# Two sets of projections as seven block products instead of eight, with the weight sums formed in the two sets before

## The chip, the cores and the metric

The kernel runs on one core of one Trainium2 chip. The metric is the device time of one execution in microseconds, taken as the median of several runs. A core has five engines with their own instruction streams: TensorE (matmuls from SBUF into PSUM), VectorE and ScalarE (elementwise work, both can read PSUM), GpSimd (elementwise work on SBUF) and SyncE, whose stream here issues nearly all DMAs. The profile calls them PE, DVE, ACT, POOL and SP; PEld is the loading of weights into TensorE.

## The reference

One inference step of a hybrid decoder layer: 2048 new positions of a prompt and 8 x 4 of samples, 1024 channels. A row-normalised input h is projected by one wide matrix, and the columns feed a short convolution and an RWKV-7 recurrence over 16 heads of 64. The two branches go through an output matrix each, are gated and added, and go through a last matrix.

```python
h = _rmsnorm(x, norm_g)
p = jnp.einsum('bsd,dn->bsn', h, w_in)            # 1024 -> 4*1024 + 4*1024 + 128 + 2*1024
xin, bg, cg, zc = _split(p_conv, CONV_SIZES)
u = cg * xin
y_c = bg * conv3(u) * jax.nn.silu(zc)
xm = p_rwkv + (prev - p_rwkv) * mu_shift          # prev: the row before
r, k, v, wd, ad, zr = _split(xm, RWKV_SIZES)
S_fin, ys = _rwkv7_scan(S0, r_h, k_h, v_h, decay, kk, a_h)
y_r = (groupnorm(ys) + bonus) * jax.nn.silu(zr)
m = jax.nn.sigmoid(gc) * (y_c @ w_out_c) + jax.nn.sigmoid(gr) * (y_r @ w_out_r)
out = x + m @ w_o                                 # then a last RMSNorm
```

The large matrices are kept in float32 accuracy by splitting both operands of each product into a high and a low part of the type fp32r: weight-high x input-high, weight-low x input-high and weight-high x input-low are added up in PSUM.

## The kernel before

**Sets.** The prompt is cut into four sets of NT = 512 positions (th = 0 to 3; LAST = 3). The last set also carries the 32 sample positions, and 8 shifted rows for the blocks that need them, so its width is 544 or 552. For a set, XH and XL (L382, L383) hold the high and low part of the normalised input, eight blocks of 128 channels (NB = 8) by the set's positions. `prep` (L749) loads four tiles of x, scales them, transposes them on TensorE and splits them (`to_cols`, L738).

**Blocks.** A `Block` (L451) is one projection to 128 output channels. There are 81 for a set: one for the low-rank inputs (`lora_block`), and for each of eight pairs of heads k, r, v, z (`rkvz_blocks`, L1002) and xin, cg, zc, bg, gc, gr (`conv_blocks`, L874). `proj` (L434) adds eight channel blocks times three split terms, 24 matmuls, into one PSUM bank of the pool ps_ip (three banks). Sets one to three do this with 512 moving columns; set four runs each block twice, with 256 and with 288 or 296 columns, as a bank holds 512. The first and last three blocks of a set run in halves as well (EDGE), so that the input of the next set can be prepared under them. The block's `evac` then reads the bank with ScalarE and VectorE.

**Weights.** In set one a weight block is loaded as 512 KB into one of four wraw buffers, ScalarE casts the high part into a whl buffer, VectorE subtracts to get the low part (`w_advance`, L390; `w_lows`, L414), and the pair of 1 MB goes back to DRAM. Sets two to four load that 1 MB straight into one of four whl buffers. `take_w` (L423) hands out the weights in the order in which the plan uses them and keeps the loads up to four blocks ahead.

**Side work.** Beside the blocks run the steps of the recurrence for each pair of heads: `rwkv_keys`, `rwkv_solve`, `rwkv_merge`, `rwkv_load`, `rwkv_chain` (eight chunks of 64, each waiting for the one before; PSUM pools ps_a with two banks, ps_b with one, ps_t with two), for the last set `rwkv_sequences`, and `rwkv_out`. Each is a generator with a kind and a stretch of the main stream over which it is spread. While the program is built, a model of the engines (`Clock`, L58) says when operands are ready, and `Side.run` (L493) lets a step go only then. So the order of each engine is fixed when the program is built, and on the chip it is only waited for. SP issues in that order too: a DMA that waits holds back those behind it.

**Merges.** Under the end of set four `merge_first` (L1497) multiplies the convolution outputs of sets one and two by w_out_c, with `load_first` (L1523) splitting them into XH and XL. Then, for each set, the remaining products with w_out_c and w_out_r and the last product with w_o follow, with weights kept in the same way.

The profile gives one line for every recorded operation, L264, because all engines are called through one helper; groups are told apart by the names of their tiles: ip is a ps_ip bank, whl a weight pair, pa, pb and pt banks of the side work.

## Time and profile before

| what | us |
|---|---|
| median of 3 runs (3165.68 to 3173.09) | 3166.51 |
| span of the profiled execution | 3166.9 |
| TensorE busy in it | 3071.6 |
| VectorE busy | 1972.5 |
| ScalarE busy | 1256.6 |
| GpSimd busy | 316.2 |

DMA moved 621.89 MB, 196 GB/s over the span. The span is that of one execution taken by the profiler; it lies 0.4 us above the median. Busy times of matmuls overlap, so a busy TensorE is not one at its peak. In a row of a group stand the engine, the operation, output and input tiles, shapes and count, then the busy time, the mean of one in ns, and the idle time of that engine just before, with what ended it. In a row of a stretch stand its length and the busy time of TensorE, its weight loads, VectorE, ScalarE and GpSimd, then TensorE's granted clock, the busy share of the DMA engines and GB/s.

### The profile page before, as it was taken

How to read it: one execution, taken by the hardware profiler on the slowest of the kernel's cores; microseconds unless marked ns; L12 is line 12 of the kernel's file. 1: busy time of each engine (PE TensorE's matmuls, PEld its weight loads, DVE VectorE, ACT ScalarE, POOL GpSimd, SP SyncE). 2: the span in 40 equal slices, each digit the busy share in tenths (PEclk: the TensorE clock that was granted, in tenths of full speed). 3: DMA queues.
4: the chain of work that ended last, by engine and by line, in shares of the span. 5: the costliest groups of instructions: out<-in, count | busy, mean ns of one | idle time of the engine just before them, and what ended most of it. 6: DMA issues, size and time to landing. Idle time of an engine off the chain costs nothing. (4 is left out here: it accounts for less than half of the span.)

```text
span 3166.9 us, 55564 instructions
## 1 busy us (share of the span) xinstructions
PE 3071.6 (97%) x21530; PEld 2630.7 (83%) x21530; DVE 1972.5 (62%) x5444; ACT 1256.6 (40%) x2583; POOL 316.2 (10%) x521
## 2 busy tenths in 40 slices
PE   7899999999999999999999999999999998999998
PEld 6678777888888888787888889998999988878896
DVE  5577777766666666666656676777677753443432
ACT  4455555544343444444444444444444431211201
POOL 2011111111111111111111110000000010000000
PEclk9899999999999999999999999999999999999999
DMA  8677777754444444444444444443444469988863
GB/s 269 234 241 234 227 226 227 239 192 162 151 164 166 166 163 162 163 163 151 161 164 164 159 152 138 149 141 131 147 148 136 165 226 313 346 324 316 315 240 120
DMA packets 252253, 621.89 MB, mean 196 GB/s; under 512 B 35210, under 2 KB 153091, under 8 KB 198230
## 3 DMA queue, kind: packets, MB, share of 16 engines
q1 hardware_dynamic: 251846, 617.82, 56.9%
q8 instruction: 170, 2.79, 0.3%
q14 instruction: 93, 0.76, 0.1%
q0 software_dynamic: 144, 0.52, 0.0%
HBM read 457.34 MB, written 160.94 MB: 195 GB/s over the span
## 5 line engine op out<-in xcount | busy, mean ns | idle before, releaser
L264 PE MATMUL ip<-XH,whl 128*128 128x512 f32 (+3 forms) x7776 | 2112.6, 352 | 34.3 <-DVE tmp L264 11.0
L264 PEld LDWEIGHTS ip<-XH,whl 128*128 128x128 f32 x7776 | 1346.6, 191 | 190.2 <-DVE whl L264 12.2
L264 PE MATMUL ip<-XL,whl 128*128 128x512 f32 (+3 forms) x3888 | 1364.7, 351 | 0.1
L264 PEld LDWEIGHTS ip<-XL,whl 128*128 128x128 f32 x3888 | 741.5, 191 | 74.5 <-issue 5.6
L264 DVE TENSOR_TENSOR tt<-Mi,X 128x60 f32<-128x60 f32 (+24 forms) x992 | 215.3, 217 | 29.9
L264 DVE TENSOR_TENSOR X<-X,tt 128x60 f32<-128x60 f32 (+24 forms) x992 | 211.7, 213 | 32.3
L264 DVE SCALAR_TENSOR_TENSOR S<-pb,pe,sp 64x64 f32<-64x64 f32 x512 | 143.6, 280 | 135.7 <-PE pb L264 128.3
L264 ACT ACTIVATE tmp<-ip,vec 128x512 f32<-128x512 f32 (+2 forms) x174 | 102.6, 592 | 281.0 <-PE ip L264 276.7
L264 ACT ACTIVATE sp<-S,pe 128x128 f32<-128x128 f32 x256 | 102.8, 402 | 265.0 <-DVE S L264 264.1
L264 ACT COPY SV<-pb 64x128 f32<-64x128 f32 x256 | 66.0, 258 | 325.0 <-PE pb L264 323.0
L264 PE MATMUL po<-whl,MH 128*128 128x512 f32 x544 | 170.4, 394 | 0.0
L264 DVE TENSOR_TENSOR UB<-pa,P 64x64 f32<-64x64 f32 x512 | 109.9, 215 | 95.8 <-PE pa L264 78.9
L264 DVE TENSOR_TENSOR whl<-wraw,whl 128x1024 fp32r<-128x1024 f32 x105 | 132.8, 1267 | 50.5 <-ACT whl L264 42.1
L264 ACT CAST whl<-wraw 128x1024 fp32r<-128x1024 f32 x105 | 108.9, 1040 | 58.9 <-PE ip L264 36.9
L264 PE MATMUL ip<-RH,whl 128*128 128x512 f32 (+2 forms) x512 | 128.4, 342 | 2.1 <-DMA whl<-w_or 1.9
L264 PEld LDWEIGHTS po<-whl,MH 128*128 128x128 f32 x544 | 102.3, 188 | 23.6
L264 ACT COPY Xbd<-Mi 32x256 f32<-32x256 f32 x128 | 88.2, 689 | 72.0 <-DVE Mi L264 69.8
L264 DVE SCALAR_TENSOR_TENSOR gt<-gt,ip 128x288 f32<-128x288 f32 (+2 forms) x67 | 36.5, 544 | 125.4 <-PE ip L264 100.8
L264 ACT ACTIVATE tmp<-ip 128x512 f32<-128x512 f32 (+2 forms) x126 | 63.0, 500 | 124.3 <-PE ip L264 124.0
L264 PEld LDWEIGHTS pb<-UB,Xbd 128*128 128x128 f32 x512 | 86.7, 189 | 30.5 <-PE ip L264 9.2
L264 PEld LDWEIGHTS pa<-S,AR 128*128 128x128 f32 x512 | 89.9, 190 | 26.5 <-DVE S L264 12.1
L264 DVE TENSOR_TENSOR GM<-pt,mask_p 128x512 f32<-128x512 f32 x128 | 82.6, 686 | 45.8 <-PE pt L264 45.6
(495 smaller groups left out, 3914.4 us busy)
## 6 DMA issues: line engine op xcount, KB each, us to landing
wraw<-in_w_in_dram SPq DMA_DIRECT2D x81, 512.0 KB
whl<-w_k SPq DMA_DIRECT2D x24, 1024.0 KB
whl<-w_r SPq DMA_DIRECT2D x24, 1024.0 KB
whl<-w_v SPq DMA_DIRECT2D x24, 1024.0 KB
whl<-w_z SPq DMA_DIRECT2D x24, 1024.0 KB
whl<-w_xin SPq DMA_DIRECT2D x24, 1024.0 KB
whl<-w_cg SPq DMA_DIRECT2D x24, 1024.0 KB
whl<-w_zc SPq DMA_DIRECT2D x24, 1024.0 KB
```

Of the source, the lines that this page charges most:

```text
L264: r = f(*a, **k)
```

## The change

Sets three and four (FAST = (2, 3)) no longer multiply block by block. Two blocks X and Y of 128 outputs, the 1024 input channels in two halves and the positions in two halves make a product of 2 x 2 by 2 x 2 blocks. Eight products of (128 outputs) x (512 channels) x (half of the positions) are replaced by seven, in the manner of Strassen and Winograd: four of them use sums S1 to S4 of weight blocks, four use sums T1 to T4 of input blocks, and three of these use both. A product is 4 channel blocks x 3 split terms, 12 matmuls with 256 columns in set three and 276 in set four (XN). The 81 blocks of a set become 40 pairs and a lora block of 60 matmuls.

- `Pair.product` runs the products of a pair in seven of the slots that SLOTS gives, with those of neighbouring pairs between. m, b and c are PSUM banks; m takes P1, P6, P7 and P4 one on top of the other and is read after each of them. Passes on ScalarE and VectorE put the four output quarters together, and the former evacuation work runs once both blocks are whole (`mixed_fin`, `inner_end`, `outer_end`, `gates_end`; `outer_end` multiplies by bg on GpSimd).
- The unit of weights is half a block, 512 KB with both parts, and whl has seven such buffers in place of four of 1 MB.
- `comb` makes the sums of weights: 12 pairs beside set one and 28 beside set two. It reloads both raw blocks, adds on GpSimd, splits on ScalarE and VectorE and stores four units.
- `xprep` makes the seven parts of a set's input (VARS) one set ahead and stores them in DRAM; `load_x_part` brings each part to its place (PLACE) as soon as the last product that reads the old one is issued. T1, T3, T4 and B22 lie in XA, the former XH and XL; B11, B21 and T2 in six of the raw buffers, of which there are now eight.
- ps_ip has four banks in place of three, and ps_a one in place of two. The last stage's pools, the order of a few small steps (new_shift, new_conv, the buffers of `rwkv_sequences`) and constants of the model change along with it. The split of the first half of yc no longer starts under the end of set four.

The core of the diff:

```diff
+NUNIT = 7
+FAST = (2, 3)
+SLOTS = {"P1": 0, "P2": 1, "P6": 3, "P5": 5, "P7": 6, "P4": 9, "P3": 11}
+HOLDS = {"P1": "B11", "P2": "B21", "P6": "T2", "P5": "T1", "P7": "T3", "P4": "T4", "P3": "B22"}
...
-    whl_p = clock.pooled(ctx.enter_context(tc.tile_pool(name="whl", bufs=4)), "whl", 4)
+    whl_p = clock.pooled(ctx.enter_context(tc.tile_pool(name="whl", bufs=NUNIT)), "whl", NUNIT)
...
-        w_advance(i + 3, i + 2, i + WAHEAD)
-        return parts_.pop(i)
+        w_advance(i + 6, i + 4, i + NUNIT)
+        return [parts_.pop(i + j) for j in range(n)]
...
-    ps_a = clock.pooled(ph1.enter_context(tc.tile_pool(name="ps_a", bufs=2, space=PSUM)), "ps_a", 2)
+    ps_a = clock.pooled(ph1.enter_context(tc.tile_pool(name="ps_a", bufs=1, space=PSUM)), "ps_a", 1)
...
+    def load_x_part(th, v):
...
+        if isinstance(at, int):
+            t = XA[:, at * NB * XW // 2:at * NB * XW // 2 + NB * n].rearrange("p (a k t) -> p a k t", a=2, t=n)
+            SP.dma_start(out=t.bitcast(F32), in_=src)
+            xv[v] = t[:, 0], t[:, 1]
+        else:
...
+            for i in range(2):
+                SP.dma_start(out=xv[v][i].bitcast(F32), in_=src[:, i])
...
+    def xprep(th):
...
+            t1, t2, t4 = (xt[:, i * n:(i + 1) * n] for i in range(3))
+            V.tensor_tensor(out=t1, in0=b11, in1=b12, op=ALU.subtract)
+            V.tensor_tensor(out=b12, in0=b22, in1=b12, op=ALU.subtract)
+            V.scalar_tensor_tensor(out=t2, in0=t1, scalar=-1.0, in1=b22, op0=ALU.mult, op1=ALU.subtract)
+            V.scalar_tensor_tensor(out=t4, in0=t2, scalar=-1.0, in1=b21, op0=ALU.mult, op1=ALU.subtract)
+            yield 1, [t4]
+            for vi, src in enumerate((b11, b12, b21, b22, t1, t2, t4)):
+                hi = rw.tile([P, XW // 2], F32R, name="xhi")[:, 0:n]
+                A.copy(hi, src)
+                V.tensor_tensor(out=src.bitcast(F32R), in0=src, in1=hi.bitcast(F32), op=ALU.subtract)
+                yield 0.5, [src, hi]
+                SP.dma_start(x_d[th][:, vi, 0, k, :], hi.bitcast(F32))
+                SP.dma_start(x_d[th][:, vi, 1, k, :], src)
...
+        def product(self, k):
...
+            u, = take_w((self.th, *self.unit(k)), 1)
+            v = HOLDS[k]
...
+            ps = self.b if k == "P2" else self.c if k in ("P5", "P3") else self.m
+            u = u.rearrange("p a (k n) -> p a k n", n=P)
+            xh, xl = xv[v]
+            for kt in range(HB):
+                for i, (w_, m_) in enumerate(((u[:, 0, kt], xh[:, kt]), (u[:, 1, kt], xh[:, kt]), (u[:, 0, kt], xl[:, kt]))):
+                    T.matmul(ps[:, :n], lhsT=w_, rhs=m_, start=kt + i == 0 and k in ("P1", "P2", "P5"),
+                             stop=kt == HB - 1 and i == 2, skip_group_check=k in ("P6", "P7", "P4", "P3"))
+                    yield n / NT / 3
+            X, Y = self.x, self.y
+            if k == "P1":
+                A.copy(X[:, h], ps[:, :n])
+            elif k == "P2":
+                V.tensor_tensor(out=X[:, h], in0=ps[:, :n], in1=X[:, h], op=ALU.add)
+                ps_ip.free(ps)
+            elif k == "P6":
+                A.copy(X[:, e], ps[:, :n])
+            elif k == "P7":
+                A.copy(Y[:, e], ps[:, :n])
+                V.scalar_tensor_tensor(out=Y[:, e], in0=self.c[:, :n], scalar=-1.0, in1=Y[:, e], op0=ALU.mult, op1=ALU.subtract)
+            elif k == "P4":
+                A.activation(out=Y[:, h], in_=ps[:, :n], func=AF.Copy, scale=-1.0)
+                ps_ip.free(ps)
+            elif k == "P3":
+                V.tensor_tensor(out=X[:, e], in0=ps[:, :n], in1=X[:, e], op=ALU.add)
+                ps_ip.free(ps)
+                self.end(X, Y)
...
+    def comb(prs, me, ahead, spare):
...
+            adds = [(u1, Y[:, h], Y[:, e]), (Y, X[:, h], Y[:, h]), (u2, u1[:, e], X[:, h]), (X, u2[:, e], X[:, e])]
+            for t, a, b in adds[0:2]:
+                G.tensor_tensor(out=t[:, e], in0=a, in1=b, op=ALU.add)
...
+            for two in (((1, u1), (3, Y)), ((2, u2), (4, X))):
+                for _, t in two:
+                    A.copy(t[:, h].bitcast(F32R), t[:, e])
+                yield 1, [t[:, h] for _, t in two]
+                for _, t in two:
+                    V.tensor_tensor(out=t[:, e].bitcast(F32R), in0=t[:, e], in1=t[:, h], op=ALU.subtract)
+                more(i)
+                yield 1, [t[:, e] for _, t in two]
+                for k, t in two:
+                    SP.dma_start(flat((f"S{k}", *pr.names[0])), t)
+                    wraw_p.free(t)
```

More of the change, by code (lines that the diff above doesn't have):

```diff
@@ L400, in w_advance @@
             i = state["split"]
-            _, src, keep, there = order[i]
-            if i >= (load if there else split):
+            _, j, src, keep, there = order[i]
+            if i >= min(load if there else split, state["dma"]):
                 break
-            hl = whl_p.tile([P, 2, NB * P], F32R, name="whl")
+            hl = whl_p.tile([P, 2, UW], F32R, name="whl")
             if there:
@@ L517, in push @@
     def push():
+        SP.flush(0)
+        if tmp.open:
+            return
         for sd in [sd for kind in ("samp", "keys", "out") for sd in live if sd.kind == kind and sd.f0 <= where[0]]:
-            if all(x.ended for x in sd.after):
+            if not sd.running and all(x.ended for x in sd.after):
                 sd.run(where[0] + 1e-6, True, True)
@@ L1540, in load_first, with units, do, g @@
             yield 1
-    EDGE = 3
+    def units(bl):
+        kind = (bl.key[0],) + bl.key[2:]
+        return [(bl.key, kind + (j,), j, bl.src) for j in range(2)]
+    def do(f, *a):
+        def g():
+            f(*a)
+            return
+            yield
+        return 0.0, g, ()
+    def product(pr, k):
+        u = pr.unit(k)
+        j = u[-1] if k in ("P1", "P2", "P4") else 0
+        return 4.0 * pr.n / NT, lambda: pr.product(k), [((pr.th, *u), u, j, None)]
+    def lora_item(th):
+        bl = lora_block(th)
+        a, c = units(bl)
+        return 60.0 * XN[th] / NT / 3, lambda: lora_fast(bl, XN[th], NTT[th]), [a, (bl.key, ("ln",), 0, None), c]
@@ new lines, in block_item, with g, items, length @@
+    def block_item(x, c0, c1):
+        def g():
+            kind = (x.key[0], x.key[1]) if x.key[0] in ("oc", "or") else ("prep", x.key[1])
+            need(*(job.get((*kind, hf)) for hf in range(2) if (c1 > HN if hf else c0 < HN)))
+            yield from x.part(c0, c1)
+        return (c1 - c0) / NT * NB, g, units(x)
+    def items(parts):
+        return [block_item(*x) for x in parts]
+    def length(its):
+        return sum(w for w, _, _ in its)
+    EDGE = 3
+    F0 = FAST[0]
+    blocks = {th: [x for b in range(NB) for x in conv_blocks(th, b)] for th in range(NSETS) if th not in FAST}
@@ new lines, in hybrid_kernel, with rested @@
+    for pr in pairs:
+        for k in ("P5", "P6", "P7", "P3"):
+            kind = pr.unit(k)
+            if kind not in scratch:
+                scratch[kind] = dram.tile([P, 2, UW], F32, name="w_" + "_".join(map(str, kind)))
+    scratch["ln",] = dram.tile([P, 2, UW], F32, name="w_ln")
+    for _, hv, _, _ in plan:
+        for _, _, us in hv:
+            for u in us:
+                keep(*u)
+    def rested(n):
+        return sum(wraw_p.ends(h) + REST <= clock.t["PE"] for h in wraw_p.open) >= n
@@ L1694, in hybrid_kernel @@
     before = None
+    sums = [pr for pr in pairs if pr.th == F0]
+    seldom = {0: sums[:12], 1: sums[12:]}
     clock.planning = True
```

525 lines of the change are left out of this document (390 added, 135 removed).

## The prediction

> **What bounds the kernel now.** First the head of the profile's page.
>
> ```profile
> span 3166.9 us, 55564 instructions
> PE 3071.6 (97%) x21530; PEld 2630.7 (83%) x21530; DVE 1972.5 (62%) x5444; ACT 1256.6 (40%) x2583; POOL 316.2 (10%) x521
> ...
> PEclk9899999999999999999999999999999999999999
> ```
>
> TensorE is busy for 97% of the span at nearly full granted clock. That alone proves little, so I cut the span by stage: start, set one, set two, set three, set four, first merge, rest. The boundaries are where the 1944 projection matmuls of 512 columns of a set (81 blocks of 24) are used up.
>
> ```profile
> core 0: us, PE busy (x) PEld busy (x) DVE busy (x) ACT busy (x) POOL busy (x), PEclk, DMA share, GB/s
> 0.00:130.00 130.00, 102.70 (x511) 84.75 (x512) 74.22 (x155) 65.11 (x103) 22.72 (x71) 0.96 0.82 273
> 130.00:647.00 517.00, 506.23 (x3342) 408.43 (x3342) 394.05 (x1000) 268.99 (x498) 68.89 (x93) 0.99 0.72 229
> 647.00:1251.00 604.00, 595.88 (x4063) 491.40 (x4062) 386.61 (x1128) 250.06 (x521) 69.71 (x118) 1.00 0.47 162
> 1251.00:1854.00 603.00, 594.21 (x4051) 489.78 (x4051) 385.42 (x1120) 250.14 (x520) 70.94 (x118) 1.00 0.47 161
> 1854.00:2574.00 720.00, 706.62 (x6415) 665.33 (x6413) 506.69 (x1608) 313.61 (x747) 64.32 (x100) 1.00 0.43 147
> 2574.00:2700.00 126.00, 114.10 (x849) 107.20 (x849) 50.81 (x86) 27.90 (x38) 6.15 (x4) 0.95 0.89 310
> 2700.00:3167.00 467.00, 451.89 (x2312) 383.79 (x2310) 174.72 (x350) 80.75 (x158) 13.50 (x17) 0.99 0.75 275
> ```
>
> Sets three and four (rows 1251 and 1854) leave TensorE idle for 8.8 and 13.4 us; VectorE, the next compute engine, is at 64 and 70% there, and the DMA engines are below half. A matmul taken out of these two rows shortens the span as long as nothing else fills up. The waits of TensorE over the whole span say the same: none adds up to 15 us.
>
> ```profile
> engine line waited for: us in total, times, longest us
> PE ip L264 <- DVE tmp L264: 14.9, 10, 8.0
> PE ip L264 <- DVE GM L264: 10.7, 1, 10.7
> PE ip L264 <- DVE whl L264: 9.6, 8, 3.5
> ```
>
> **The matmuls removed.** A matmul's busy time overlaps its neighbour's, so the price is the distance of starts in the timeline of TensorE, for 512, 296 and 256 columns:
>
> ```profile
> 1505.57 0.62 PE L264 MATMUL ip<-XH,whl 128*128 128x512 f32 x2
> ...
> 1508.37 0.63 PE L264 MATMUL ip<-XH,whl 128*128 128x512 f32 x2
> ...
> 2207.36 0.44 PE L264 MATMUL ip<-XH,whl 128*128 128x296 f32 x2
> ...
> 2208.18 0.44 PE L264 MATMUL ip<-XH,whl 128*128 128x296 f32 x2
> ...
> 2208.59 0.40 PE L264 MATMUL ip<-XH,whl 128*128 128x256 f32 x2
> ...
> 2209.65 0.28 PE L264 MATMUL ip<-XH,whl 128*128 128x256 f32 x1
> ```
>
> Twelve of 512 take 2.80 us (233.3 ns), six of 296 take 0.82 us (136.7 ns), nine of 256 take 1.06 us (117.8 ns). The line through 256 and 296 gives 133 ns at 288 and 127.3 ns at 276, the width in set four afterwards.
>
> Set three before: 1944 x 233.3 = 453.5 us. After: 40 pairs x 7 products x 12 matmuls, and 60 for the lora block, 3420 x 117.8 = 402.9 us. Set four before: each block is a part of 256 and one of 296 (33 blocks) or 288 (48), 1944 x (117.8 + 134.5) = 490.5 us. After: 3420 x 127.3 = 435.4 us. The gain is 50.6 + 55.1 = **105.7 us**. The transposes of x move from prep to xprep, 32 a set in both; no recurrence matmul changes. Nothing lies under these matmuls that could be uncovered at once: the next bounds are DMA and VectorE.
>
> The Trainium skill (TensorE: Matmul & The Clock Gate, Back-to-back issue gap) speaks against this: it says the spacing is set by the weight load as well as the matmul, with 81 ns at 128 columns and 131 ns at 512. A line through these would put 256 at 98 ns, 0.75 of the 512 figure, an estimate from that page; then 84 narrow matmuls would cost as much as 63 wide ones in place of 48 and the change would lose. The trace disagrees for this type: 117.8 of 233.3 ns is 0.505.
>
> **What is added, and its cover.** Prices of elementwise work, from the groups by form:
>
> ```profile
> L264 DVE SCALAR_TENSOR_TENSOR tmp<-tmp,ip 128x256 f32<-128x256 f32 x32 | 13.1, 418 | 30.5 <-PE ip L264 15.6 <-DMA tmp<-gc 12.6 <-ACT tmp L264 2.2
> L264 ACT ACTIVATE tmp<-ip 128x256 f32<-128x256 f32 x36 | 13.8, 383 | 30.3 <-PE ip L264 30.1
> L264 DVE SCALAR_TENSOR_TENSOR ML<-gt,MH 128x512 fp32r<-128x512 f32 x21 | 14.5, 691 | 12.0 <-ACT MH L264 12.0
> L264 POOL TENSOR_TENSOR tmp<-tmp,bv 128x512 f32<-128x512 f32 x24 | 30.9, 1286 | 87.5 <-ACT tmp L264 87.5
> L264 ACT CAST whl<-wraw 128x1024 fp32r<-128x1024 f32 x105 | 108.9, 1040 | 58.9 <-PE ip L264 36.9 <-DMA wraw<-in_w_o_dram 8.3 <-DMA wraw<-in_w_out_r_dram 6.8
> ```
>
> Each pair adds three VectorE and four ScalarE passes of 256 columns: 40 x 3 x 0.418 = 50 us and 40 x 4 x 0.383 = 61 us a set. The bg multiply goes to GpSimd (-5.5 us of VectorE). Set four drops the second part of its evacuations, about 72 instructions, each worth 2 x 0.418 - 0.69 = 0.15 us (-11 us). The sums cost 4 x 0.69 us of VectorE and 4 x 1.286 us of GpSimd a weight pair: 33 and 62 us for 12 pairs in set one, 77 and 144 us for 28 pairs in set two; xprep's 44 passes at 0.418 us stand against prep's twelve at 0.69, some 10 us more in sets two and three. VectorE's share becomes 427/517 = 0.83, 474/604 = 0.78, 440/554 = 0.79, 536/665 = 0.81 in sets one to four (before 0.76, 0.64, 0.64, 0.70).
>
> What does a busier VectorE cost TensorE? In the stage rows TensorE idles 1.4% where VectorE is at 0.64, 1.9% at 0.70 and 2.1% at 0.76, 6 points for 100. At the new shares that is +2, +5, +5 and +4 us, **16 us**; between 0 (the planner places work ahead) and 30 (twice the slope, GpSimd's adds taking their turns with VectorE).
>
> DMA. A unit is 512 KB; a whole block was 1 MB:
>
> ```profile
> wraw<-in_w_in_dram SPq DMA_DIRECT2D x81, 512.0 KB
> whl<-w_k SPq DMA_DIRECT2D x24, 1024.0 KB
> ...
> 80.00:100.00 20.00, 15.97 (x62) 12.04 (x61) 8.93 (x12) 9.29 (x15) 0.39 (x3) 0.91 1.00 359
> 2880.00:2920.00 40.00, 39.84 (x172) 31.72 (x171) 13.09 (x19) 4.55 (x8) 0.00 (x0) 1.00 0.83 306
> 2920.00:2960.00 40.00, 40.00 (x174) 32.39 (x173) 13.83 (x21) 6.24 (x11) 0.00 (x0) 1.00 0.86 322
> ```
>
> Set three moves 161 x 603 = 97 MB. It loses 81 x 1.05 = 85 MB and gains 283 units = 148 MB, xprep's stores of seven parts (8 MB) and some 12 MB of part loads: 180 MB in 554 us, 326 GB/s. Set two: 98 MB and 28 pairs x (1.05 read + 2.1 written) = 88 MB, parts 10 MB: 196 MB in 604 us, 325 GB/s. Set one: 118 + 12 x 3.15 = 156 MB in 517 us, 302 GB/s. Set four: 169 MB in 665 us, 254 GB/s. From below, the rows at 2880 show 306 and 322 GB/s with TensorE busy for 79.84 of 80 us. From above, the first merge at 310 GB/s has TensorE idle 9.4% of the time, 8% more than a set. Loads straight from scratch make up set three and the rows at 2880 alike, so I take 1% of sets two and three and half that of set one: **14 us**, ends 0 and 0.08 x 1675 = 134.
>
> The Trainium skill (DMA: Bandwidth & Descriptors, Specifications) gives about 358 GB/s of HBM bandwidth a core. By it sets two and three would sit at 91% of the limit, an estimate from that page, and nothing would be lost on average; the trace agrees as far as it goes, since the row at 80 reads 359 GB/s at a full share, with TensorE idle for 4 of 20 us.
>
> SP is one queue in order. A part of x can be fetched only when the last product that reads its place is done, and loads of weights issued later stand behind that wait. Into set three, T1, T3, T4, B22 (4 MB, some 12 us at 322 GB/s) are due after three to seven products of 1.41 us, with other work between; into set four all seven parts go one by one over 18 slots (some 36 us) with 9 MB of weights, 17 MB in all, 52 us at 322 GB/s, less 6 units held ahead. I take **8 us** for both, ends 0 and 20. After set four the first half of yc can't be split beneath the last blocks any more, since XA is read to the end: one cast of 1.04 us and one subtraction of about 1.27 us stand bare, with their handovers **4 us**, ends 2 and 8.
>
> At nothing I cost: one ps_a buffer instead of two. The copies that read it end long before the next group of chunks writes it:
>
> ```profile
> L264 PE MATMUL pa<-S,AR x6: 272/274/276, 1530.4 to 1542.5; 128*128 128x128 f32 x6
> ...
> L264 ACT COPY Yc<-pa x2: 367/368/370, 1539.1 to 1539.5; 64x256 f32<-64x256 f32 x2
> ```
>
> The copies end at 1539.9, the next matmul into pa starts at 1542.5, 2.6 us later. If ScalarE ran that much later, each of 32 pairs would pay the excess. A product's bank is written again two products later (2.8 us) against one 0.38 us evacuation; the GpSimd multiplies hide behind 88% idle GpSimd.
>
> **Sum.** -105.7 + 16 + 14 + 8 + 4 = -63.7. The span 3166.9 is 0.4 above the median of 3166.51, so the forecast is 3166.9 - 63.7 = 3103.2, **3103 us**.
>
> **Rivals.** (1) All additions hide but the two handovers: 3167 - 106 + 6 = 3067. For it: the idle of sets two to four is 1 to 2% whatever runs beside; against: at DMA share 0.89 the first merge idles 12 of 126 us. (2) DMA comes to its limit where the sums are made. Set one's mix of narrow reads and stores moves 229 GB/s at share 0.72, so 318 at full share; 196 MB of set two then take 616 us, over its 604, and set three's 180 MB 566 us, over its 554: about 12 us each in place of the 6 taken, and bursts as much again: with set one 40 us in place of 14, and 10 more at the set changes, 3140. (3) **Slower:** prefetching breaks down, TensorE running dry in sets one to three as in the first merge, since all waits and loads share SP's queue. 134 in place of 14 gives 3223; it decides the sign once DMA waits pass 78 us (4.6% of the 1675 us of these sets), half of the way. Against it: six units of lead are over 8 us of matmuls. (4) The weight load binds at 256 columns: at the 190 ns of one load, 6840 x 0.190 = 1300 us in place of 944, 3520 us. The timeline excludes it unless new operands behave otherwise.
>
> ```profile
> L264 PEld LDWEIGHTS ip<-XH,whl 128*128 128x128 f32 x2594 | 418.0, 190 | 9.1 <-issue 4.8 <-ACT tmp L264 0.8
> ```
>
> The Trainium skill's rule above (Back-to-back issue gap) is a milder form of (4) and has no chance beyond it, since the trace disagrees. (5) The products run, but the planner's later side work fills the freed time, so the span stays within 10 us of before: 3160.
>
> **How the numbers follow.** Forecast 0.46 (3080 to 3125), (1) 0.17, (2) 0.19 (3125 to 3157), (3) 0.11, (4) 0.01, (5) 0.06. A measurement tells 0.3% (9.5 us) from no change, that is 3157 to 3176. Faster: 0.46 + 0.17 + 0.19 = 0.82; same 0.06; slower 0.12. The range leaves out (3), (4) and the lowest tail: 3060 to 3160.
>
> **What would show it.** Starts of 256-column matmuls 118 ns apart and 127 at 276; set three near 560 us, set four near 672, sets one and two longer by under 10 each; TensorE's waits on whl loads under 20 us; DMA share 0.85 to 0.95 in sets one to three; the Yc copies ending before pa is written. Wrong would be: spacing above 125 ns, waits on DMA above 40 us, or sets one and two longer by over 25 us each.

## The result and the profile after

The changed kernel takes 3482.31 us (median of 4 runs, 3472.27 to 3499.64) against 3169.80 us for the kernel before on the same chip (4 runs, 3165.68 to 3173.54): 1.099 times as long, 95% interval 1.097 to 1.101, or 313 us more. The forecast was 3103 us, with 3160 as the upper end of the range. It was wrong in sign.

The head of the profile's page after the change, to be read beside the one of before:

```profile
span 3474.8 us, 60899 instructions
PE 3173.8 (91%) x22322; PEld 2733.7 (79%) x22322; DVE 2245.1 (65%) x5968; ACT 1460.9 (42%) x3137; POOL 569.7 (16%) x697
...
PEclk9999989999999999899999999989998999999999
...
DMA packets 480531, 906.69 MB, mean 261 GB/s; under 512 B 51948, under 2 KB 274277, under 8 KB 479210
```

TensorE is now idle for 9% of the span in place of 3%. The digits of PEclk hide how often the clock falls, since 9 stands for 90% or more: by the trace its mean is below full in 31 of the 40 slices, before in 8. TensorE's busy time rose by 102 us although it has less to multiply. Most of that is seen in sets one and two, where it multiplies as before: it was granted half the clock there for 195 us in place of 24, and is busy for 87 us more (half of the difference is 85). The span by stage, cut as before: start, sets one to four, first merge, rest (the boundaries lie where the projection matmuls of a set are used up):

```profile
core 0: us, PE busy (x) PEld busy (x) DVE busy (x) ACT busy (x) POOL busy (x), PEclk, DMA share, GB/s
0.00:16.00 16.00, 4.70 (x19) 3.81 (x19) 8.04 (x27) 9.58 (x16) 13.93 (x50) 1.00 0.71 231
16.00:715.00 699.00, 634.26 (x3834) 504.96 (x3834) 521.24 (x1252) 357.26 (x713) 145.03 (x165) 0.95 0.80 271
715.00:1464.00 749.00, 655.98 (x4030) 523.22 (x4030) 512.87 (x1298) 323.45 (x662) 230.99 (x231) 0.92 0.78 261
1464.00:2080.00 616.00, 579.77 (x5289) 550.15 (x5288) 417.00 (x1245) 301.46 (x682) 84.94 (x125) 0.97 0.82 281
2080.00:2873.00 793.00, 724.59 (x5875) 657.04 (x5875) 546.09 (x1645) 347.05 (x819) 76.96 (x109) 0.93 0.67 223
2873.00:3036.00 163.00, 153.68 (x1122) 136.59 (x1122) 81.39 (x172) 47.71 (x93) 5.40 (x3) 1.00 0.87 300
3036.00:3475.00 439.00, 420.86 (x2159) 357.89 (x2158) 158.51 (x332) 74.40 (x155) 12.47 (x17) 0.99 0.76 272
```

Measured with one rule for all kernels (a set runs from its first projection matmul to that of the next, the first merge to the first matmul into po), the stages took in us:

| kernel | set one | set two | set three | set four | first merge | rest |
|---|---|---|---|---|---|---|
| before | 627 | 604 | 604 | 722 | 155 | 435 |
| after | 699 | 749 | 616 | 792 | 163 | 439 |
| difference | +72 | +146 | +12 | +70 | +8 | +4 |

So 218 of the some 310 us are lost in sets one and two, whose products were not changed at all. Put beside them were the sums of weights and, in set two, `xprep` for set three; the buffers changed as well. Sets three and four, with some 105 us of matmul time taken out, became longer too. Of the prediction's own signs of being wrong, one came in, sets one and two longer by over 25 us each; the other two, a spacing of the matmuls above 125 ns and waits on DMA above 40 us, did not. What TensorE waits for instead:

```profile
engine line waited for: us in total, times, longest us
PE pt L271 <- DVE Yc L271: 52.3, 24, 4.9
PE pb L271 <- DVE UB L271: 37.0, 32, 4.7
PE pa L271 <- DVE S L271: 31.5, 30, 3.8
PE pt L271 <- ACT tmp L271: 28.5, 20, 3.3
PE pb L271 <- ACT SV L271: 24.5, 18, 4.2
...
PE ip L271 <- DMA whl<-w_S_k: 5.4, 1, 5.4
```

These are not waits for weights, which forecast and rivals (2) and (3) looked for. They are the handovers of the recurrence: Yc, UB, S and SV are made by VectorE and ScalarE between two matmuls of a chain. What holds these up is to be seen in the timeline of all engines in set two:

```profile
start us, us, engine line op out<-in xcount [idle before <-releaser]
...
897.38 4.67 POOL L271 TENSOR_TENSOR wraw<-wraw 128x512 f32<-128x512 f32 x3 [2.57 <-DMA x<-wraw]
...
897.90 0.94 PE L271 MATMUL ip<-XA,whl 128*128 128x512 f32 x3
...
898.74 0.62 ACT L271 CAST wraw<-wraw 128x512 fp32r<-128x512 f32 x1 [3.49 <-POOL wraw L271]
...
899.29 1.63 DVE L271 SCALAR_TENSOR_TENSOR tmp<-rT,rkh,tmp 128x512 f32<-128x512 f32 x1
900.41 0.62 ACT L271 CAST wraw<-wraw 128x512 fp32r<-128x512 f32 x1 [1.05 <-POOL wraw L271]
...
902.08 0.62 ACT L271 CAST wraw<-wraw 128x512 fp32r<-128x512 f32 x1 [1.05 <-POOL wraw L271]
902.08 2.37 DVE L271 TENSOR_TENSOR wraw<-wraw 128x512 fp32r<-128x512 f32 x2 [1.16 <-POOL wraw L271]
...
902.73 0.26 ACT L271 COPY SV<-pb 64x128 f32<-64x128 f32 x1
...
903.04 0.79 PE L271 MATMUL pb<-SV,BKt 128*128 128x128 f32 x2 [4.20 <-ACT SV L271]
```

GpSimd adds three times in a row. ScalarE stands 3.49 us for the first addition, casts, stands 1.05 us for the next, casts, stands again. Behind these casts in its queue waits the copy SV, 0.26 us of work, and behind SV the matmul of the recurrence, with all the projection matmuls queued after it: TensorE stands for 4.20 us. Meanwhile the VectorE instruction at 899 us takes 1630 ns beside a running addition; before, between 700 and 1450 us, it took 752 on average (group by form):

```profile
L264 DVE SCALAR_TENSOR_TENSOR tmp<-rT,rkh,tmp 128x512 f32<-128x512 f32 x10 | 7.5, 752 | 0.4
```

Both things, the order of the queues and the slower VectorE, are taken apart below.

### The profile page after: what moved, and what is told of

Same layout as the page of the kernel before. It is cut to its first block, busy times and chain, and to the rows that moved or that the text cites. A ratio compares the mean times of both kernels' runs of the same rounds, so it can differ in the third digit from the quotient of the medians.

```text
span 3474.8 us, 60899 instructions
## 1 busy us (share of the span) xinstructions
PE 3173.8 (91%) x22322; PEld 2733.7 (79%) x22322; DVE 2245.1 (65%) x5968; ACT 1460.9 (42%) x3137; POOL 569.7 (16%) x697
## 4 chain that ended last, share of the span: by engine, by line
PE 40%; DVE 20%; issue 8%; DMA 5%; ACT 4%; POOL 3%; SPq 0%; DVEq 0%; POOLq 0%; ACTq 0%
PE ip L271 27%; PE pt L271 7%; DVE tt L271 4%; DVE X L271 4%; PE po L271 3%; PE pb L271 2%; ACT tmp L271 2%; DVE tmp L271 2%; DVE wraw L271 2%; POOL wraw L271 1%; DMA x<-xhi 1%; DVE Mi L271 1%; PE pa L271 1%; ACT Xbd L271 1%; DVE Yc L271 1%
## 5 line engine op out<-in xcount | busy, mean ns | idle before, releaser
L271 PE MATMUL ip<-XA,whl 128*128 128x512 f32 (+3 forms) x9504 | 1921.6, 348 | 41.3 <-DVE whl L271 13.5
L271 PEld LDWEIGHTS ip<-XA,whl 128*128 128x128 f32 x9504 | 1485.7, 196 | 212.3 <-DVE whl L271 19.2
L271 PE MATMUL ip<-xs,whl 128*128 128x256 f32 (+1 forms) x2952 | 460.3, 298 | 4.0 <-DVE kT L271 3.3
L271 PEld LDWEIGHTS ip<-xs,whl 128*128 128x128 f32 x2952 | 399.0, 194 | 9.6 <-DVE kT L271 3.7
L271 POOL TENSOR_TENSOR wraw<-wraw 128x512 f32<-128x512 f32 x160 | 227.2, 1428 | 143.6 <-DMA wraw<-in_w_in_dram 59.5
L271 DVE TENSOR_TENSOR whl<-wraw,whl 128x512 fp32r<-128x512 f32 x210 | 146.2, 721 | 65.6 <-ACT whl L271 65.1
L271 ACT CAST whl<-wraw 128x512 fp32r<-128x512 f32 x210 | 120.5, 617 | 71.5 <-DMA wraw<-in_w_in_dram 24.7
L271 DVE TENSOR_TENSOR wraw<-wraw 128x512 fp32r<-128x512 f32 (+3 forms) x177 | 130.8, 760 | 29.4 <-POOL wraw L271 21.6
L271 PE MATMUL pb<-UB,Xbd 128*128 128x128 f32 x512 | 113.3, 304 | 38.0 <-DVE UB L271 37.0
L271 PE MATMUL pt<-AR,BK 64*128 64x128 f32 x1056 | 128.1, 312 | 3.1 <-DVE bv L271 1.1
```

The costliest lines, as they stand in the source:

```text
L271: r = f(*a, **k)
```

## The experiments

The theory after the result: the sums cost the time, by way of the engines they share with the recurrence; the products do what was worked out. Its rivals: the weights come late; the products are slower than they look; the room that had to be given up for them (buffers) is what costs. All ratios are to the kernel before on the same chip, whose median lay between 3166 and 3170 us.

### The buffers: sz and ps_a

To make room, sz (two tiles of the last step of a pair) went from three buffers to two, and a pair waits for the output of the second pair before it in place of the third. The forecast had no term for it. In the kernel before, this alone:

```diff
-            need(job.get(("out", th * NB + p - 3)))
+            need(job.get(("out", th * NB + p - 2)))
...
-            sz = ep.tile([P, NT + NSAMP], F32, name="sz", bufs=3)
+            sz = ep.tile([P, NT + NSAMP], F32, name="sz", bufs=2)
```

> The kernel before with one part of the change alone: two sz buffers in place of three, so that z_end forces rwkv_out of two pairs back to its end. Theory A (forced output steps: TensorE stands in order behind a step whose VectorE and GpSimd work isn't done, and each stand costs half-clock time besides): slower by 20 to 60 us, all of it in set one, where the plan forces six steps; sets two and three as before. Theory B (the sums' GpSimd adds hold VectorE, and ScalarE and VectorE stand in order behind the sums) and theory C (DMA traffic dries TensorE): no change, within 5 us.

Measured 3197 us, 1.009 (1.0075 to 1.0105): 28 us by the ratio, nearly all in set one (627 to 656 us). The reverse in the changed kernel, with six half units of weights in place of seven for the room:

> The changed kernel with three sz buffers and the old distance of three pairs; room for it comes from six whl units in place of seven. Theory A: the forced output steps go in all four sets, 3482 falls by 110 to 200 us, to 3280 to 3370, with TensorE's waits on Yc below 15 us (52.3 after). Theory B: sets one and two keep most of their 67 and 146 us, and 3420 or more is left. Theory C: slower than 3482, as the lead of the weights is shorter.

Measured 3438 us, 1.085 (1.083 to 1.088): 44 us back. That is far from the 110 to 200 us by which forced output steps would explain the result, and in the range given for the sums (3420 or more). In the changed kernel it is mostly set four that gains (some 42 us, and 15 in set one, while set two gets 14 longer), and a half unit of weights went with it. So the third buffer is worth some 30 to 45 us, in another place in each kernel. The one bank of ps_a, costed at nothing, was tried by itself in the kernel before:

```diff
-    ps_a = clock.pooled(ph1.enter_context(tc.tile_pool(name="ps_a", bufs=2, space=PSUM)), "ps_a", 2)
+    ps_a = clock.pooled(ph1.enter_context(tc.tile_pool(name="ps_a", bufs=1, space=PSUM)), "ps_a", 1)
```

> The kernel before with one ps_a bank in place of two. By the gap of 2.6 us between the copies and the next matmul: 3170 within 5. If the second bank hid a wait: 1 us a pair, 3195 or more.

Measured 3172 us, 1.0006 (0.9996 to 1.0016): nothing, as costed.

### No sums at all

P5, P6, P7 and P3 read plain halves of blocks in place of the sums, so as many units are loaded and multiplied, and `comb` does not run:

```diff
-            return {"P1": (*x, 0), "P2": (*x, 1), "P4": (*y, 1)}.get(k) or ({"P5": "S1", "P6": "S2", "P7": "S3", "P3": "S4"}[k], *x)
+            return {"P1": (*x, 0), "P2": (*x, 1), "P4": (*y, 1)}.get(k) or {"P5": (*y, 0), "P6": (*x, 0), "P7": (*x, 1), "P3": (*y, 1)}[k]
...
-    seldom = {0: sums[:12], 1: sums[12:]}
+    seldom = {0: [], 1: []}
```

> The changed kernel without comb: no weight sums are made, and P5, P6, P7 and P3 read plain weight halves in place of S1 to S4 (28 + 12 pairs of loads, adds, splits and stores left out; sets three and four do the same work). Theories B and C: set one falls from 699 to about 640 us and set two from 749 to about 615, sum near 3290. Theory A: sets three and four stay at 616 and 793 us, set one keeps six forced steps, and the sum is above 3380.

> Both: three sz buffers (six whl units) and no sums. A and B together: 3110 to 3180, near or below the 3170 of before, with sets one and two at 635 and 615 us. A alone: the same as with three sz buffers and the sums. C: sets three and four, whose loads of weights are unchanged, still stand at 616 and 793 us.

Measured 3247 us, 1.027 (1.023 to 1.030), and with three buffers of sz 3214 us, 1.015 (1.013 to 1.016). The sums cost 3438 - 3214 = 224 us. With three buffers of sz and no sums, sets one and two are back at 617 and 607 us (627 and 604 before), so the loss there came from these two. But even so the kernel is some 45 us slower than before, where the sums and the buffers as the only causes would have left 3110 to 3180 us. That rest lies in set four and the first merge.

### Which part of the sums

From the kernel without sums (three buffers of sz) the parts of `comb` were put back one by one: the loads and stores alone (raw blocks are stored in place of sums); then the 160 additions, without the splits into high and low.

> The run with three sz buffers (3438), in comb only the DMAs: the raw blocks are loaded as before and four units of 512 KB a pair stored, straight from the raw buffers; the adds and the splits are left out. Between 3438 with all of the sums and 3214 with nothing of them. Theory C (DMA traffic): above 3380. Theory B (the arithmetic on GpSimd, ScalarE and VectorE): below 3260.

> The run with three sz buffers; in comb the DMAs and the 160 adds on GpSimd, without the 160 casts on ScalarE and 160 subtractions on VectorE (each unit is stored twice from its sum). Between 3276 (DMAs alone) and 3438 (all). Theory B1 (the adds' hold on VectorE is most of the 162 us): 3360 or more. Theory B2 (the splits, standing in order behind the adds, are most of it): 3330 or less.

Measured 3276 us, 1.033 (1.031 to 1.035), and 3359 us, 1.060 (1.058 to 1.062). The first lies between the answers of its expectation (below 3260, above 3380), the second 1 us below "3360 or more". With the splits it is new_sz3. The steps are 62 us for the transfers, 83 us for the additions, 79 us for the splits. The additions cost TensorE 83 us, though GpSimd is idle for four fifths of the time. Moved to VectorE, the engine that was thought to be the next bound:

```diff
-                G.tensor_tensor(out=t[:, e], in0=a, in1=b, op=ALU.add)
+                V.tensor_tensor(out=t[:, e], in0=a, in1=b, op=ALU.add)
```

> The run with three sz buffers (3438), the 160 adds of comb on VectorE in place of GpSimd. If it is GpSimd's adds that hold VectorE (B1), 90 to 160 us go although VectorE has 110 us more to do: 3280 to 3350, with sets one and two near 660 and 660 us. If it is the amount of work on VectorE and ScalarE (B2), the time rises above 3438. C: no change.

Measured 3352 us, 1.057 (1.056 to 1.059): 86 us less than with the additions on GpSimd, and only 76 more than with the transfers alone, additions and splits together. That leaves three ways in which an addition on GpSimd costs: it slows VectorE down; GpSimd's own small steps stand behind it; the stores stand behind it on SP's queue. Two runs take them apart. In the first the 160 additions are made into spare buffers that nobody reads. In the second GpSimd is kept busy as long by fills, which read nothing:

```diff
+            for t, a, b in ((u1, Y[:, h], Y[:, e]), (u2, X[:, h], X[:, e])):
+                G.tensor_tensor(out=t[:, e], in0=a, in1=b, op=ALU.add)
...
+            for t in (u1, u2, u1):
+                G.memset(t, 0.0)
```

> The kernel of sz3_sums_dma_only (3276), with the 160 additions on GpSimd made beside it into two spare buffers that nobody reads; the raw blocks are stored in place of the sums, so no store, no ScalarE and no VectorE instruction waits for an addition. sz3_sums_adds_only, where the stores wait for the additions, took 3359. If a running addition itself holds back VectorE and GpSimd's own later work, most of the 83 us comes back: above 3330. If it was the stores and loads that stood on SP's queue behind the additions, the median stays within 20 us of 3276.

> As sums_adds_unread, but with six fills of 128 x 1024 (about 0.93 us each by the 1052 ns of a fill of 1152) a pair in place of the four additions, so that GpSimd is busy about as long (5.6 us a pair against 5.7) without reading two operands. If an addition costs time because it holds VectorE's two-input instructions, the fills cost little: the median lies within 25 us of sz3_sums_dma_only (3276), and the tt and X instructions of the solve have no durations above 1 us beyond those of before. If GpSimd's own later work, delayed behind the additions, is the cost, it comes out as dear as the additions: above 3330.

Measured 3326 us, 1.050 (1.048 to 1.052), and 3274 us, 1.034 (1.032 to 1.037); the transfers alone took 3276. The first fell short of its "above 3330" by 4 us and so lies between the two answers: of the 83 us, 50 come from additions that nobody waits for, the other 33 from the stores that wait for them (and from the order that follows). The fills cost nothing. So it isn't GpSimd's time. The fills differ in two ways, though: they read nothing, and they wait for no load, while GpSimd waits 135 us for raw blocks before the unread additions. If that held up GpSimd's other work, the engines would wait longer for GpSimd. Up to 1464 us they don't: VectorE waits 11.7 us for it with unread additions and 13.0 with the transfers alone, TensorE and ScalarE not at all, and SP 59 and 45 us. What does change is VectorE's own time. Summed shape by shape over sets one and two, against the means of the run with the transfers alone, its instructions take 72 us longer with the unread additions and 27 with the fills (half of those 27 in one kind of copy, shown at the end). So what costs is what an addition does to VectorE. The groups of both kernels, first GpSimd's and then the two VectorE instructions of the solve, first with additions and then with fills:

```profile
L271 POOL TENSOR_TENSOR wraw<-wraw 128x512 f32<-128x512 f32 x160 | 220.2, 1399 | 176.8 <-DMA wraw<-in_w_in_dram 134.9 <-DVE whl L271 28.7 <-DVE GM L271 12.4
L271 DVE TENSOR_TENSOR tt<-Mi,X 128x60 f32<-128x60 f32 (+24 forms) x992 | 229.2, 231 | 28.8
L271 DVE TENSOR_TENSOR X<-X,tt 128x60 f32<-128x60 f32 (+24 forms) x992 | 227.8, 230 | 31.6
```

```profile
L271 POOL MEMSET wraw<- 128x1024 f32 x240 | 226.5, 962 | 113.4 <-DVE whl L271 49.3 <-DMA gr<-tmp 22.8 <-DVE wraw L271 18.6
L271 DVE TENSOR_TENSOR X<-X,tt 128x60 f32<-128x60 f32 (+24 forms) x992 | 213.7, 215 | 31.5
L271 DVE TENSOR_TENSOR tt<-Mi,X 128x60 f32<-128x60 f32 (+24 forms) x992 | 211.8, 213 | 28.7
```

GpSimd is busy for 220 and 226 us, and the solve's instructions are 15 to 18 ns longer on average with additions than with fills. A mean hides how: up to 1460 us the trace has 31 of 1025 of them above 1 us with additions and 2 of 1054 with fills, at a median of 216 and 215 ns. All 31 start while GpSimd is at a two-input instruction of 1.25 to 1.35 us, 29 times one of the additions, and end 45 to 93 ns after it: an instruction of 0.2 us that meets a running addition takes what is left of it. The Trainium skill (SBUF — State Buffer, SBUF: two separate sides) states this as a lock on a shared port pair: a VectorE instruction with two SBUF inputs and a GpSimd instruction that reads SBUF exclude each other for the whole instruction. The two runs agree for such instructions, the exception for GpSimd work that reads nothing included.

### The planner's order of the sums

The planner's model of the engines already counts that a GpSimd instruction and a VectorE instruction with two SBUF inputs shut each other out. The change exempts the additions (the kind comb): they are planned as if VectorE were never held by them or they by it. That exemption undone:

```diff
-        if eng == "POOL" and self.kind != "comb" or eng == "DVE" and sum(ap.space != PSUM for ap in ins) > 1:
+        if eng == "POOL" or eng == "DVE" and sum(ap.space != PSUM for ap in ins) > 1:
```

> The run with three sz buffers (3438); the planner's rule that a GpSimd instruction and a two-input VectorE instruction don't run at once is applied to the sums too, as to all other work; the change had exempted them. If leaving them out of the plan is what makes TensorE stand (the order is right for a chip without the hold): below 3400. If the hold itself is the loss wherever the adds are put: 3438 within 25, or above.

Measured 3480 us, 1.096 (1.094 to 1.099): 42 us slower than with the exemption (3438), 32 of them in set three (602 to 634 us). So the cost isn't that the model leaves the holds out. Why the loss falls in set three, beside which no sums are made, isn't shown; that the additions kept apart push other work back in the plan is a guess.

### Sets three and four without sums

What remains is that sets three and four and the first merge took 604 + 722 + 155 = 1481 us before and 600 + 754 + 173, some 1526 us, without sums, though TensorE has some 105 us less to do there. First three edits on that kernel: the pairs k/r and v/z after those of the convolution, with a tenth tmp buffer; three VectorE passes a pair left out; two buffers for kT and rT, with five half units.

```diff
-                runs.append(((th, p), cs[:2] + rkvz(th, p + 1) + cs[2:], None))
+                runs.append(((th, p), cs + rkvz(th, p + 1), None))
...
-                V.tensor_tensor(out=X[:, h], in0=ps[:, :n], in1=X[:, h], op=ALU.add)
...
-        kinds = {"k": (RW0 + D, NB + p, al("kT", 1, "keys", 1), put("k")), "r": (RW0, p, al("rT", 1, "keys", 1), put("r")),
+        kinds = {"k": (RW0 + D, NB + p, al("kT", 2, "keys", 2), put("k")), "r": (RW0, p, al("rT", 2, "keys", 2), put("r")),
```

> The run with three sz buffers and no sums (3214); in sets three and four the k, r, v, z pairs come behind the convolution pairs instead of after two of them, and there are ten tmp buffers in place of nine. Theory D (sets three and four don't gain because k and r need their one buffer before rwkv_keys of the pair before is done, so its steps are forced): 3160 to 3190, sets three and four together 25 to 50 us shorter than 600 + 754. Theory E (VectorE has too much to do there): within 12 us of 3214.

> The run with three sz buffers and no sums (3214); in sets three and four the three VectorE passes of each pair are left out (P2, P3 and P7 aren't added to the other quarter; the ScalarE passes stay). 50 us less of VectorE a set. Theory E: 3214 falls by 40 us or more. Theory D: by less than 20.

> Without sums, three sz buffers, the k, r, v, z pairs late (3192), and two buffers each for k and r in place of one; room comes from five whl units and nine tmp buffers. Theory D (forced rwkv_keys in set four): set four falls from 754 us to below 725, and the time to 3165 or less even with some us lost in the merges for the two units. Theory E (VectorE's and ScalarE's amount of work): set four stays above 740. Theory C (lead of the weights): slower in every set, above 3215.

Measured 3192 us, 1.007 (1.005 to 1.009); 3187 us, 1.006 (1.004 to 1.007); 3209 us, 1.012 (1.011 to 1.014). The first gained 23 us in sets three and four (25 to 50 expected), the second 27 us in all, between its two answers (under 20, 40 or more); the third brought set four below 725 us as expected, but not the time to 3165. By stage (sums from unrounded times):

| kernel | set three | set four | first merge | sum |
|---|---|---|---|---|
| before | 604 | 722 | 155 | 1481 |
| new_sz3_nosums | 600 | 754 | 173 | 1526 |
| nosums_late_keys | 577 | 754 | 174 | 1505 |
| nosums_fewer_passes | 598 | 729 | 177 | 1503 |
| nosums_two_kr | 590 | 675 | 263 | 1528 |
| old_half_solve | 597 | 708 | 153 | 1459 |
| nosums_late_half_solve | 574 | 723 | 169 | 1466 |
| nosums_two_kr_half_solve | 585 | 681 | 186 | 1452 |

The row of nosums_two_kr is telling: with room for the keys of two pairs, set four takes 675 us, what was forecast (672), and the first merge grows by 90 us. The recurrence of the last set doesn't end earlier, it ends under the merge instead, and TensorE waits for it there. The row of that merge:

```profile
2513.00:2776.00 263.00, 209.17 (x1442) 176.82 (x1441) 145.04 (x363) 82.59 (x168) 11.49 (x11) 0.85 0.65 217
```

TensorE stands for 54 of the 263 us while VectorE is busy for 55% of them, ScalarE for 31% and the DMA engines for 65%. No engine's amount of work is the limit there; it is work that waits for other work. That calls for a test of the recurrence itself. The solve of each pair is cut from 31 steps to 15, in the kernel before as a control and in two of the new ones:

```diff
-        for j in range(31, 0, -1):
+        for j in range(15, 0, -1):
```

> The kernel before, in which the solve of each pair runs 15 of its 31 steps, j from 15 down (16 x 2 VectorE instructions a pair are left out, so the inverses are not complete). By the rows of before one such instruction takes about 212 ns, so 8 pairs x 32 x 0.212 = 54 us of VectorE a set. If TensorE's own matmuls are the bound of the kernel before, its sets stay near 604 and 722 us and the median within 1% of 3169. If the side work of the recurrence bounded it already, it falls by 50 us or more.

> The kernel without sums and with the late keys (3192), with the same cut of the solve as in old_half_solve. Theory that the recurrence's side work is the next bound in sets three and four: sets three and four fall from 577 and 754 us by 60 us or more together, the median to about 3110 to 3130, while the old kernel hardly moves. Theory that the distance of the products or the reads of their banks hold TensorE up: sets three and four stay within 15 us, the median stays above 3175. Theory that the weights run dry: no change.

> The kernel without sums, late keys, two buffers for kT and rT and five half units (3209), with the same cut of the solve. Side work as the bound: the first merge, which had grown to 263 us because the recurrence of set four ended under it, shrinks by 40 us or more, set four stays near 675 us, and the median falls to about 3110 to 3140. If the first merge is held by loads instead, it stays above 250 us and the median above 3180.

Measured 3127 us, 0.987 (0.9855 to 0.988); 3130 us, 0.988 (0.986 to 0.9895); 3124 us, 0.986 (0.984 to 0.987). The cut is worth 42 us in the kernel before, between the two answers of its expectation (1.3%, and under 50 us); 62 us with late keys; 86 us with two buffers of kT and rT, 77 of them in the first merge (263 to 186 us). With late keys sets three and four fell by 34 us together, not by the 60 expected, and set three by 3 of them. So the recurrence binds set four and the first merge more than it did in the kernel before, where it was a part of the bound already; for set three it wasn't shown. The merge of 186 us also shows that it wasn't the five half units that made it 263. One rival is left in set four: the shorter solve also takes 54 us from VectorE and gave 31 us there (754 to 723), and 50 us of VectorE's passes left out gave 25 (754 to 729). Whether it is the chains' length or VectorE's amount of work that these two cuts relieve, they don't tell.

## Why the prediction was wrong

Stacked from the runs, in the order in which the pieces were put on:

| step | median, us | step, us | forecast's term |
|---|---|---|---|
| before | 3169 | | |
| products, without sums, sz of three | 3214 | +45 | -105.7, with the set changes, yc, VectorE's passes and most transfers |
| the sums' loads and stores | 3276 | +62 | part of 14 for all transfers |
| 160 additions that nobody reads | 3326 | +50 | within 16 for VectorE |
| stores waiting for the additions | 3359 | +33 | none |
| splits on ScalarE and VectorE | 3438 | +79 | within 16 for VectorE |
| sz from three buffers to two (and seven half units) | 3482 | +44 | none |

**The matmuls: right.** Starts lie 119 and 128 ns apart in the changed kernel (median; 117.8 and 127.3 worked out), so rival (4) is out. In the run with three sz buffers and no sums, the median distance times the number of projection matmuls is 407 us in set three (402.9 worked out, 453 before) and 438 us in set four (435.4, and 490 before), 99 us less than before. By the mean of the distances under 400 ns at full clock it is 111 us less. So about 105 us did leave TensorE's work.

**What that was worth: wrong.** The step that failed first is the sentence that nothing lies under these matmuls that could be uncovered at once, with DMA and VectorE as the next bounds, read from busy shares. The chains of the recurrence lie under them, each with its turns TensorE - VectorE - TensorE - ScalarE, on engines that look free: in sets three and four without sums VectorE is busy for 70% of the time and ScalarE for 51 and 46%. The projection matmuls were the cover under which these turns took place. With some 105 us of cover gone and the products' own passes in the same queues, they came to light: without sums sets three and four and the first merge took some 45 us more, not 105 less. For set four and the merge the shorter solve shows this; for set three it is argued. Nearest to that is rival (5), which had 0.06. Between -105 and +45 lie some 150 us. The forecast had a small part of them, for the products' passes, the set changes and yc; other parts are traced: the order of the pairs gave back 22 us (3214 to 3192), three passes a pair on VectorE 27 us (3214 to 3187), the shorter solve 20 to 44 us more than in the control. These need not add up, and the rest is open; in set three 14 of the 574 us stay above the forecast of 560 with late keys and a short solve.

**The idle time of TensorE per point of VectorE's share: wrong in kind.** The 16 us came from a slope through three stages of one kernel (6 points of idle time for 100 of VectorE). In set two VectorE's share is 513/749 = 0.68 after the change, hardly above the 0.64 of before, and TensorE lost 146 us there. VectorE's time there, 513 us, is 39 more than the 474 worked out; its instructions of sets one and two take 62 us longer in new_sz3 than with the transfers alone, shape by shape. But 39 us of VectorE don't make 146. What stands in front of a handover on a queue, and how long that may take, counts too. The splits (79 us) put instructions that wait for GpSimd into the in-order queues of ScalarE and VectorE; the timeline at 897 us shows three casts ahead of SV. That the waiting is the larger part of the 79 us isn't shown, but with the additions on VectorE, where no split waits for GpSimd, additions and splits together cost 76 us. A slip without effect: the terms for VectorE in set four add up to 540 us, not 536, a share of 0.81 either way.

**GpSimd at nothing: wrong.** The prediction worked out 62 and 144 us of additions on GpSimd and gave them no term of their own. They cost 83 us, 50 of them with nobody waiting for their results. The upper end of 30 us that the prediction gave to additions "taking their turns with VectorE" named the mechanism and undersized it.

**DMA: the size was off, not the bounds.** The sums' transfers alone cost 62 us against 14 for all transfers (ends 0 and 134), 43 of them in set two. Rival (2) put 40 there for a bandwidth limit. But the stages don't look like one: TensorE's waits for DMAs come to 10 us in sets one and two together, 8 of them in one wait. In set two of sz3_sums_dma_only it waits most for UB and S:

```profile
PE pb L271 <- DVE UB L271: 9.6, 12, 1.7
PE pa L271 <- DVE S L271: 7.1, 8, 2.4
PE pb L271 <- ACT SV L271: 3.6, 6, 1.4
```

Nor do late loads of the recurrence show: in that stage VectorE doesn't wait for a DMA at all (0.8 us without the transfers), ScalarE for 11 us (25), and GpSimd for 30 (7), 27 of them in one wait. Whether the plan orders the work less well around the new steps was not tried, so the cause of the 62 us is open. The set changes and yc, 12 us together, can't be told from the rest; the first merge is 8 us longer after the change.

**Buffers: an edit not costed.** The prediction went through ps_a and found no cost, rightly. It passed over sz, whose third buffer is worth 28 us in the kernel before and, with a half unit of weights given up for it, 44 in the new one. Both were in the diff in the same way.

No version was found that is faster than the kernel before. The best that computes all of it is sz3_sums_on_vector, 3352 us. Even a kernel that got its sums for nothing would stand at 3192 (late keys). Only with the recurrence cut in half does it come level with the control: 3124 against 3127 us.

## What to carry to other kernels

Before taking matmuls out of a kernel whose TensorE is full, ask which chains of short turns between engines run beneath them, and how long these would take with nothing above: their length can be the next bound where no engine's busy share shows it, and a control that shortens them in the old kernel tells whether they bind already. Side work on an idle engine is free only if it doesn't lengthen the instructions of an engine that matters, and if nothing waiting for it stands in an in-order queue ahead of a handover. Cost every buffer count that the diff lowers, one by one.

## What was not expected of the hardware

An addition of 128 x 512 on GpSimd (1.4 us) can make a VectorE instruction of 0.22 us with two SBUF inputs last up to 1.34 us, while a fill of GpSimd does next to nothing to such an instruction (the tile's durations, first with additions, then with fills):

```profile
L271 DVE TENSOR_TENSOR tt<-Mi,X x513: 160/215/1340, 102.4 to 1459.9; 128x60 f32<-128x60 f32 x17, 128x28 f32<-128x28 f32 x12, 128x66 f32<-128x66 f32 x11, 128x48 f32<-128x48 f32 x10
```

```profile
L271 DVE TENSOR_TENSOR tt<-Mi,X x527: 160/215/1308, 104.7 to 1415.1; 128x60 f32<-128x60 f32 x17, 128x28 f32<-128x28 f32 x12, 128x66 f32<-128x66 f32 x12, 128x48 f32<-128x48 f32 x11
```

The two maxima are alike, since the kernel has other two-input work on GpSimd as well; it is their number, 31 against 2, that differs.

Fills are not harmless to every VectorE instruction. A copy of 128 x 2 from SBUF to SBUF, 0.17 us in the median, lasted 10.04 us under a row of twelve fills, and the S of a chain behind it 6.68 us:

```profile
L271 DVE COPY u<-ucar x18: 116/169/10043, 56.0 to 1405.8; 128x2 f32<-128x2 f32 x18
```

These copies are few, and the kernel's time did not show it.

A short stand also costs more than its own length. The trace's record of the granted clock has 11 spells at half clock before, 56 us of the span, and 49 after, 351 us of it, none shorter than 3.41 us. Most of those after the change follow a stand of 1 to 5 us. In set two, where TensorE was idle for 93 of 749 us, the clock was low for 120 us, and the stage's mean is 0.92 (1.00 before). The Trainium skill (TensorE: Matmul & The Clock Gate, Part 1) gives a window of about 3.4 us for the gate, which the length of the spells agrees with; by the page a whole window of idle time drops the clock, and here stands of 1.0 to 1.5 us were followed by a spell too. Not every stand is: after 20 of the 62 above 1.5 us none came within 7 us.
